# Expert rows stored already scaled by norm_moe, w1 and w3 loaded two rows per partition, and another arena order, in a two-block transformer kernel

## Chip, cores and metric

The kernel runs on one core of one Trainium2 chip, as one launch. The metric is the device time of that launch in microseconds; the time of a version is the median of several runs. Lower is better.

## What is computed

Two transformer blocks follow each other on 1024 rows of 1024 float32 numbers. The first has a gated linear recurrence and a differential attention side by side, and then a mixture of 32 experts, of which each row takes two. The second has sliding-window and forgetting attention and a plain MLP. The part that is changed is the mixture of experts, which in the reference comes to this:

```python
xn = rms_norm(x, norm_moe)                      # x * rsqrt(mean(x*x) + eps) * norm_moe
g_sel, e_in_group = router(xn)                  # top-1 group, top-2 experts of 8 in it
for e in range(32):                             # rows tok with weights w, packed by expert
    hid = silu(xn[tok] @ w1[e]) * (xn[tok] @ w3[e])     # 1024 -> 512
    out[tok] += (hid @ w2[e]) * w                       # 512 -> 1024
x = x + out
```

## The kernel before, in words

The program is written as tasks (Python generators) with priorities. A planner runs them: class `Model` holds assumed costs, `Tasks.run` takes the task of the highest priority whose data are due, and `Later` holds an instruction of ACT, DVE or POOL back until its operands are due by the model. So the order on each engine is a result of the planner, not of the text. Every matmul is issued in the helper's line 234, every ACT, DVE and POOL operation in line 270, plain DMAs in 221 and indirect ones in 227; in the profile the tile names tell the operations apart.

Products are made in three matmuls (`mm3`): each float32 operand is cut into a high part (float32r) and the rest. Weights come through one stream (`Stream`): a 512-KB piece is loaded from HBM into a raw buffer, cut (`split`: an ACT copy of 128x1024 makes the high part, a DVE subtract of 128x1024 the rest), and then used by PE. The raw buffers lie in the arenas `exact` (F) and two `swing` arenas, the cut ones in `rounded` (R). A load is issued when a raw buffer is free, a cut when a cut buffer is.

Phase `mix` (line 1297) multiplies the mixed branches with w_out, adds x and gets eight tiles of 128 rows. It stores each tile twice: to `XR` (d_xr), from which the experts' rows are gathered, and to `X1` (d_x), to which the experts' results are added by scatter. Meanwhile the router and the routing tables are computed.

Phase `moe` (line 1637) goes through the experts in the order of `moe_order` (line 605). For expert e, `hidden` takes the eight pieces of w1 and w3, 48 matmuls of 128x512; `xform` for the next expert turns the 128 gathered rows (eight transposes of 128x128 into PSUM) and cuts them into th and tl; `outputs` for the expert before takes four pieces of w2, 24 matmuls and a scatter; `turn` makes four transposes of the hidden rows. The gain norm_moe is applied in `xform`: after the transposes it is one number per partition (`self.gm`, one column for each 128 rows of the weights), so each 128x128 block has an ACT activation with that scale and a DVE scalar_tensor_tensor with it (`split_T`, line 653). The factor rsqrt of each row is applied later in `hidden` (`rt`). `gather` (line 1648) is an indirect DMA on POOL from XR. During the first experts DVE and PE also make the index tables of the later ones. `overflow` (line 1816) handles experts with more rows than one tile; its loop isn't entered here.

A piece of w1 or w3 holds 256 rows of 512 numbers; in `w_unit` (line 794) partition p gets rows p and 128+p, two runs of 2 KB. A piece of w2 holds 128 rows of 1024, one run of 4 KB for each partition.

Of the kernel before, what the change touches and what calls it, by code (L numbers as in the profile page):

```python
# [10 lines left out]
F32 = mybir.dt.float32  # L11
# [8 lines left out]
D = 1024  # L20
# [592 lines left out]
class Kern:  # L613
    def __init__(self, ctx, tc, io, out, stop=None):
# [5 lines left out]
        ps = ctx.enter_context(tc.tile_pool(name="ps", bufs=1, space=bass.MemoryType.PSUM))  # L620
        self.dram = ctx.enter_context(tc.tile_pool(name="dr", bufs=1, space=bass.MemoryType.DRAM))
        self.sz = ctx.enter_context(tc.tile_pool(name="sz", bufs=1, reuse_waits="tile"))
        self.R = Arena(sb.tile([128, NR], F32R, name="rounded"), NR, F32R)
        self.Z, self.turns = [None, None], 0
        for i in range(2):
            self.swing(i, F32R)
        self.F = Arena(sb.tile([128, NF], F32, name="exact"), NF, F32)
        self.psum = ps.tile([128, 4096], F32, name="psum")
# [165 lines left out]
    def w_unit(self, w, c0, n=512, k0=0, nk=8, kk=2):  # L794

        return [self.ws.add([(0, n, w[(k0 + i) * 128:(k0 + i + kk) * 128, c0:c0 + n].rearrange("(a p) c -> p a c", p=128))],
                            (kk, n)) for i in range(0, nk, kk)]

    def w_unit2(self, w, cols, nk=8, kk=2):

        out = []
        for i in range(0, nk, kk):
            at, srcs = 0, []
            for c, n in cols:
                srcs.append((at, n, w[i * 128:(i + kk) * 128, c:c + n].rearrange("(a p) c -> p a c", p=128)))
                at += n
            out.append(self.ws.add(srcs, (kk, at)))
        return out

    def plan(self):  # L810
# [15 lines left out]
        for kind, e in moe_order():  # L826
            if kind == "h":
                U["h"][e] = [self.w_unit(w[e], 0, k0=2 * i, nk=2)[0] for i in range(4) for w in (w1, w3)]
            if kind == "y":
# [467 lines left out]
    def mix(self):  # L1297
# [6 lines left out]
        self.x1 = Slots(F, 2, 1024)  # L1304
        self.x1ready = {}
        tb = Banks(self.psum, 4, 2)
        banks = Banks(self.psum, 0, 4)
# [46 lines left out]
        for half in range(2):  # L1354
# [39 lines left out]
            for tt in range(4 * half, 4 * half + 4):  # L1394
                b = yield from self.x1.take()
                self.sp.dma_start(b.f(), io["x"][0, tt * 128:(tt + 1) * 128])
                for u in range(2):
# [15 lines left out]
                    self.x1ready[tt, u] = b  # L1413
                for z in (self.XR, self.X1):
                    self.sp.dma_start(z[tt * 128:(tt + 1) * 128], b.f())
        mixT.free()
        self.swing(1, F32)
        self.ws.grow(raw=[self.Z[1].alloc(1024) for _ in range(2)])
# [218 lines left out]
    def moe(self):  # L1637
# [46 lines left out]
        def xform(e):  # L1684
# [3 lines left out]
            for c in range(2):  # L1688
                p = tb.next()
                self.transposes(p, x.f()[:, c * 512:c * 512 + 512], 4)  # L1690
                for j in range(4):
                    k = 4 * c + j
                    s = slice(k * 128, k * 128 + 128)
                    self.split_T(p[:, j * 128:j * 128 + 128], th.r()[:, s], tl.r()[:, s], th.f()[:, s], self.gm[:, k:k + 1])
            XT[e] = th.r(8, 128), tl.r(8, 128)
# [120 lines left out]
    def overflow(self, hl, th, tl, hT):  # L1816
# [29 lines left out]
        with tc.For_i(0, count, 1) as j:  # L1846
# [8 lines left out]
            for c in range(2):  # L1855
                p = self.bank(4 + c)
                transposes(p, xg.f()[:, c * 512:c * 512 + 512], 4)
                for i in range(4):
                    k = 4 * c + i
                    s, q, g = slice(k * 128, k * 128 + 128), p[:, i * 128:i * 128 + 128], self.gm[:, k:k + 1]  # L1860
                    act.activation(th.r()[:, s], q, AF.Copy, scale=g)
                    v.scalar_tensor_tensor(tl.r()[:, s], q, g, th.f()[:, s], op0=OP.mult, op1=OP.subtract)
            xh, xl = th.r(8, 128), tl.r(8, 128)
            for i in range(4):
                for n, w in enumerate((io["w1"], io["w3"])):
                    wh, wl = weights(w[0][bass.ds(e, 1), 256 * i:256 * i + 256].rearrange("o (a p) c -> p (o a) c", p=128), (2, 512))
                    for q in range(2):
# [759 lines left out]
```

## Time and profile before

| | |
|---|---|
| median of 3 runs | 2845.98 us (2844.07 to 2849.95) |
| the profiled execution | 2842.55 us |
| its span | 2840.6 us |
| mean granted TensorE clock | 0.981 |
| busy share | PE 95%, DVE 61%, ACT 53%, POOL 15% |
| DMA | 492.57 MB, mean 173 GB/s |

The span is from the first instruction to the last of one execution taken by the profiler; the execution's own time is a little longer. The experts take the stretch from about 932 to 1550 us of it; before it lies the first block's attention, behind it the second block. Times within the trace are counted from the start of the span. An idle time "[x <-E]" in a row is how long that engine had stood before it, and which engine's instruction ended the wait.

### The profile page before, as it was taken

How to read it: one execution, taken by the hardware profiler on the slowest of the kernel's cores; microseconds unless marked ns; L12 is line 12 of the kernel's file. 1: busy time of each engine (PE TensorE's matmuls, PEld its weight loads, DVE VectorE, ACT ScalarE, POOL GpSimd, SP SyncE). 2: the span in 40 equal slices, each digit the busy share in tenths (PEclk: the TensorE clock that was granted, in tenths of full speed). 3: DMA queues.
4: the chain of work that ended last, by engine and by line, in shares of the span. 5: the costliest groups of instructions: out<-in, count | busy, mean ns of one | idle time of the engine just before them, and what ended most of it. 6: DMA issues, size and time to landing. Idle time of an engine off the chain costs nothing. (4 is left out here: it accounts for less than half of the span.)

```text
span 2840.6 us, 37526 instructions
## 1 busy us (share of the span) xinstructions
PE 2692.9 (95%) x13162; PEld 2163.3 (76%) x13162; DVE 1738.8 (61%) x3243; ACT 1505.1 (53%) x2596; POOL 437.1 (15%) x486
## 2 busy tenths in 40 slices
PE   8899999999999899999998898899999999999999
PEld 6677787778777677788876776677777778888887
DVE  4474443643565798999997647846666665434333
ACT  4144444643443777899887646635545554243332
POOL 0540002420121232111111322200000100000000
PEclk9999999999999899999999999999999999999999
DMA  5322223335546898999997544353244433432321
GB/s 182 115 92 90 90 72 114 119 112 184 182 163 249 300 316 309 362 356 350 354 349 271 177 143 136 120 178 123 82 137 144 137 120 125 147 94 89 104 89 60
DMA packets 303023, 492.57 MB, mean 173 GB/s; under 512 B 30224, under 2 KB 127152, under 8 KB 302832
## 3 DMA queue, kind: packets, MB, share of 16 engines
q1 hardware_dynamic: 291136, 467.58, 48.2%
q0 software_dynamic: 9216, 16.81, 2.4%
q10 hardware_dynamic: 2480, 5.77, 0.5%
q8 instruction: 104, 1.70, 0.2%
q14 instruction: 87, 0.71, 0.1%
HBM read 436.38 MB, written 70.45 MB: 178 GB/s over the span
## 5 line engine op out<-in xcount | busy, mean ns | idle before, releaser
L234 PE MATMUL psum<-rounded,swing 128*128 128x512 f32 (+1 forms) x3840 | 945.0, 398 | 22.0 <-DVE exact L270 9.9
L234 PEld LDWEIGHTS psum<-rounded,swing 128*128 128x128 f32 x3840 | 704.1, 191 | 186.3 <-issue 17.7
L234 PE MATMUL psum<-swing,rounded 128*128 128x512 f32 (+2 forms) x3328 | 798.3, 393 | 0.0
L234 PE MATMUL psum<-rounded 128*128 128x512 f32 (+4 forms) x3456 | 750.6, 388 | 34.6 <-DVE rounded L270 15.3
L234 PEld LDWEIGHTS psum<-swing,rounded 128*128 128x128 f32 x3328 | 606.1, 189 | 141.3 <-issue 7.7
L234 PEld LDWEIGHTS psum<-rounded 128*128 128x128 f32 (+1 forms) x3456 | 572.9, 190 | 183.1 <-DVE rounded L270 23.6
L270 DVE TENSOR_TENSOR rounded<-exact,rounded 128x1024 fp32r<-128x1024 f32 (+2 forms) x477 | 557.2, 1191 | 239.9 <-ACT rounded L270 220.6
L270 ACT ACTIVATE rounded<-exact 128x1024 fp32r<-128x1024 f32 (+2 forms) x477 | 485.0, 1045 | 338.0 <-PE psum L234 291.8
L234 PE MATMUL psum<-exact 128*128 128x128 f32 (+5 forms) x2198 | 312.1, 284 | 79.1 <-DVE exact L270 23.3
L270 POOL TENSOR_TENSOR exact<-exact 128x1 f32<-128x1 f32 (+6 forms) x272 | 263.8, 973 | 714.4 <-DMA exact<-d_cb 287.6
L234 PEld LDWEIGHTS psum<-exact 128*128 128x128 f32 (+2 forms) x2198 | 261.8, 163 | 143.5 <-DVE exact L270 37.6
L270 ACT ACTIVATE exact<-psum 128x512 f32<-128x512 f32 (+4 forms) x282 | 155.2, 551 | 389.9 <-PE psum L234 322.1
L270 ACT ACTIVATE exact<-exact 128x512 f32<-128x512 f32 (+11 forms) x430 | 267.4, 632 | 166.1 <-DVE exact L270 136.8
L270 DVE TENSOR_TENSOR exact<-psum,exact 128x512 f32<-128x512 f32 x184 | 126.7, 688 | 200.9 <-PE psum L234 169.0
L270 DVE TENSOR_TENSOR rounded<-swing,rounded 128x1024 fp32r<-128x1024 f32 x196 | 228.9, 1217 | 11.9 <-ACT rounded L270 11.8
L270 ACT ACTIVATE rounded<-swing 128x1024 fp32r<-128x1024 f32 x196 | 201.1, 1089 | 26.1 <-PE psum L234 18.4
L270 DVE CUSTOM_DVE_ANT_0 exact<-psum,exact 128x512 f32<-128x512 f32 (+5 forms) x224 | 127.7, 592 | 71.1 <-PE psum L234 49.4
L270 POOL TENSOR_SCALAR exact<-exact 128x1 f32<-128x1 f32 (+4 forms) x134 | 41.7, 311 | 802.1 <-DVE exact L270 551.6
L270 DVE TENSOR_TENSOR swing<-psum,swing 128x512 fp32r<-128x512 f32 (+2 forms) x151 | 89.0, 615 | 90.1 <-ACT swing L270 89.8
L227 POOL DMA_INDIRECT d_x<-exact x31 | 67.3, 2172 | 482.3 <-ACT exact L270 482.3
L270 DVE TENSOR_TENSOR exact<-exact 128x512 f32<-128x512 f32 (+9 forms) x206 | 109.5, 538 | 46.9 <-POOL exact L270 24.0
L270 ACT ACTIVATE exact<-psum,exact 128x512 f32<-128x512 f32 (+1 forms) x174 | 95.2, 600 | 71.6 <-PE psum L234 60.9
(43 smaller groups left out, 1157.2 us busy)
## 6 DMA issues: line engine op xcount, KB each, us to landing
swing<-in_w_dram SPq DMA_DIRECT2D x192, 512.0 KB, 11.0
exact<-in_w_dram SPq DMA_DIRECT2D x181, 512.0 KB, 10.2
exact<-in_w_in_dram SPq DMA_DIRECT2D x72, 512.0 KB, 4.5
exact<-in_w_up_dram SPq DMA_DIRECT2D x64, 512.0 KB, 3.9
exact<-in_w_down_dram SPq DMA_DIRECT2D x64, 512.0 KB, 3.5
exact<-in_w_out_dram SPq DMA_DIRECT2D x32, 512.0 KB, 4.9
exact<-in_x_dram SPq DMA_DIRECT2D x16, 512.0 KB, 5.9
d_g<-exact SPq DMA_DIRECT2D x32, 256.0 KB, 2.3
```

The source lines that it names most:

```text
L227: r = fn(*args, **kw)
L234: r = fn(*args, **kw)
L270: r = fn(*args, **kw)
```

## The change

Four things are changed.

The arena `exact` moves to a pool of its own behind the swing arenas. Its size and use stay.

The rows of XR are stored multiplied with norm_moe. `mix` loads norm_moe once to all partitions (`xgain`, 512 KB) and multiplies every row tile on DVE (128x1024) into a new buffer `xgr` before the store to XR. X1 gets the plain rows as before. So `xform` no longer applies a gain, and cuts 512 columns at a time: two ACT copies and two DVE subtracts of 128x512 for an expert, in place of eight and eight of 128x128.

A piece of w1 or w3 is loaded so that partition p gets rows 2p and 2p+1, one run of 4 KB (`w_pair`). The k-th part of the sum then runs over the even or the odd rows of a block of 256. To match, XR's columns are stored in that order (`pairs`): within each 256, first the even ones, then the odd ones.

`overflow` is changed in the same way. `xgain` and `xgr` hold 2048 columns of `exact` during `mix`; in the experts' phase the stream has 24 raw buffers where it had 25. On POOL the order is the same.

The core of the diff (`overflow` left out):

```diff
@@ __init__ @@
+        self.R = Arena(sb.tile([128, NR], F32R, name="rounded"), NR, F32R)
         self.sz = ctx.enter_context(tc.tile_pool(name="sz", bufs=1, reuse_waits="tile"))
-        self.R = Arena(sb.tile([128, NR], F32R, name="rounded"), NR, F32R)
         self.Z, self.turns = [None, None], 0
         for i in range(2):
             self.swing(i, F32R)
-        self.F = Arena(sb.tile([128, NF], F32, name="exact"), NF, F32)
+        sf = ctx.enter_context(tc.tile_pool(name="sf", bufs=1))
+        self.F = Arena(sf.tile([128, NF], F32, name="exact"), NF, F32)
...
+    def w_pair(self, w, k0):
+
+        return self.ws.add([(0, 512, w[k0:k0 + 256].rearrange("(p a) c -> p a c", a=2))], (2, 512))
...
-                U["h"][e] = [self.w_unit(w[e], 0, k0=2 * i, nk=2)[0] for i in range(4) for w in (w1, w3)]
+                U["h"][e] = [self.w_pair(w[e], 256 * i) for i in range(4) for w in (w1, w3)]
@@ mix @@
+        self.xgain, xgr = F.alloc(1024), Ring(F, 1, 1024)
+        self.sp.dma_start(self.xgain.f(), self.row_bcast(io["norm_moe"], D))
+        pairs = lambda z: z.rearrange("p (i q a) -> p i a q", a=2, q=128)
...
-                for z in (self.XR, self.X1):
-                    self.sp.dma_start(z[tt * 128:(tt + 1) * 128], b.f())
+                xg = xgr.next()
+                v.tensor_tensor(xg.f(4, 2, 128), pairs(b.f()), pairs(self.xgain.f()), OP.mult)
+                self.sp.dma_start(self.XR[tt * 128:(tt + 1) * 128], xg.f())
+                self.sp.dma_start(self.X1[tt * 128:(tt + 1) * 128], b.f())
         mixT.free()
+        self.xgain.free()
+        xgr.free()
@@ moe, xform @@
                 p = tb.next()
-                self.transposes(p, x.f()[:, c * 512:c * 512 + 512], 4)
-                for j in range(4):
-                    k = 4 * c + j
-                    s = slice(k * 128, k * 128 + 128)
-                    self.split_T(p[:, j * 128:j * 128 + 128], th.r()[:, s], tl.r()[:, s], th.f()[:, s], self.gm[:, k:k + 1])
+                s = slice(c * 512, c * 512 + 512)
+                self.transposes(p, x.f()[:, s], 4)
+                self.split(p, th.r()[:, s], tl.r()[:, s], th.f()[:, s])
```

Since the planner sets the order, these are three places at which it differs.

The first is ACT while the experts' tables are made, at one of five experts at which it stood in this way. `rounded` from `psum` is xform's or turn's high part, `rounded` from `exact` or `swing` a piece of weights; the brackets name the engine or queue whose semaphore is waited for. Before:

```order
L270 ACTIVATE swing_6227<-psum,exact 128x512
L270 ACTIVATE rounded<-psum,exact 128x128 [waits PE_49]
L270 ACTIVATE rounded<-psum,exact 128x128 [waits DVE_49] x3
L270 ACTIVATE rounded<-psum,exact 128x128 [waits PE_49]
L270 ACTIVATE rounded<-psum,exact 128x128 [waits DVE_49] x3
L270 ACTIVATE rounded<-exact 128x1024 [waits DMAHW2_49,PE_49,Activation_49]
L270 ACTIVATE rounded<-exact 128x1024 [waits DMAHW3_49,PE_49,Activation_49]
L270 ACTIVATE rounded<-swing_6227 128x1024 [waits DMAHW4_49,PE_49,Activation_49]
L270 ACTIVATE rounded<-swing_6227 128x1024 [waits DMAHW5_49,PE_49,Activation_49]
L270 ACTIVATE exact<-psum,exact 128x512 [waits DMASW6_49]
L270 ACTIVATE exact<-psum,exact 128x512
L270 ACTIVATE rounded<-psum 128x512 [waits PE_49]
```

and now:

```order
L270 ACTIVATE swing_6241<-psum,exact 128x512
L270 ACTIVATE rounded<-exact 128x1024 [waits DMAHW2_49,DVE_49,PE_49]
L270 ACTIVATE rounded<-psum 128x512 [waits PE_49] x2
L270 ACTIVATE rounded<-swing_6241 128x1024 [waits DMAHW3_49,DVE_49,PE_49]
L270 ACTIVATE rounded<-swing_6241 128x1024 [waits DMAHW4_49,DVE_49,PE_49]
L270 ACTIVATE rounded<-swing_6241 128x1024 [waits DMAHW5_49,DVE_49,PE_49]
L270 ACTIVATE exact<-psum,exact 128x512 [waits DMASW2_49,PE_49]
L270 ACTIVATE exact<-psum,exact 128x512 [waits PE_49]
L270 ACTIVATE rounded<-psum 128x512 [waits PE_49]
```

Of xform's rows (128x128 with `psum`, now the pair of 128x512), three of each four activations waited for DVE; the two that stand now wait for PE alone.

The second is SP at the last row tile of `mix`; the loads of weights stand between the stores to d_xr and d_x. Before:

```order
L221 DMA exact<-in_w_dram 128x1024 x4
L221 DMA swing_6227<-in_w_dram 128x2x512 x2
L221 DMA d_xr<-exact 128x1024
L221 DMA d_x_4488<-exact 128x1024
L221 DMA exact<-in_w_dram 128x2x512
L221 DMA swing_5792<-in_w_dram 128x2x512 x6
```

and now:

```order
L221 DMA swing_6241<-in_w_dram 128x1024 x2
L221 DMA d_x_4491<-exact 128x1024
L221 DMA exact<-in_w_dram 128x1024
L221 DMA d_xr<-exact 128x1024
L221 DMA swing_5800<-in_w_dram 128x1024 x6
```

The store to d_xr now stands behind the store to d_x and one more load.

The third is DVE at the same tile. Before:

```order
L270 TENSOR_TENSOR exact<-psum,exact 128x512
L270 TENSOR_TENSOR rounded<-exact,rounded 128x1024
L270 SCALAR_TENSOR_TENSOR exact<-exact 128x1
L270 RECIPROCAL exact<-exact 128x1
L270 TENSOR_TENSOR exact<-exact 128x1
L270 TENSOR_SCALAR exact<-exact 128x32 x2
L270 TENSOR_TENSOR exact<-exact 128x1
L270 TENSOR_TENSOR exact<-exact,psum 128x96
```

and now:

```order
L270 TENSOR_TENSOR exact<-psum,exact 128x512
L270 TENSOR_TENSOR rounded<-exact,rounded 128x1024
L270 SCALAR_TENSOR_TENSOR exact<-exact 128x1
L270 TENSOR_TENSOR exact<-exact 128x1024
L270 TENSOR_TENSOR exact<-exact 128x1
L270 RECIPROCAL exact<-exact 128x1
L270 TENSOR_TENSOR exact<-exact 128x1
L270 TENSOR_SCALAR exact<-exact 128x32 x2
L270 TENSOR_TENSOR exact<-exact,psum 128x96
```

The multiply exact<-exact of 128x1024 stands between the steps of the last tile's routing.

Beside these, nine transposes in the second block's attention on PE, which stood behind 21 matmuls of one product, now stand behind 66; some 150 us later the rows are the same again.

## Rows read from the trace of the kernel before

**Rows 1.** Windows: stage, its length, busy time of each engine, TensorE clock, DMA, GB/s.

```profile
1002.00:1157.00 155.00, 138.80 (x621) 111.23 (x620) 138.75 (x237) 114.77 (x168) 35.37 (x15) 0.94 0.88 309
1157.00:1405.00 248.00, 248.00 (x1178) 206.31 (x1177) 238.57 (x309) 226.25 (x336) 42.38 (x28) 1.00 0.99 358
1405.00:1517.00 112.00, 108.75 (x504) 87.40 (x503) 100.06 (x131) 95.01 (x144) 17.04 (x11) 1.00 0.98 356
1850.00:2310.00 460.00, 442.80 (x2234) 351.90 (x2233) 288.44 (x576) 234.03 (x435) 26.63 (x43) 0.98 0.43 133
```

**Rows 2.** PE in time, steady expert: start, duration, operation, count, idle before.

```profile
1157.11 1.04 PE L234 MATMUL psum<-exact 128*128 128x128 f32 x8
...
1163.80 11.15 PE L234 MATMUL psum<-rounded 128*128 128x512 f32 x48
1174.79 1.03 PE L234 MATMUL psum<-exact 128*128 128x128 f32 x8
```

**Rows 3.** PE in time, 1002 to 1157 us.

```profile
1001.67 1.04 PE L234 MATMUL psum<-exact,swing 128*128 128x128 f32 x8
...
1077.21 0.66 PE L234 MATMUL psum<-exact 128*128 128x48 f32 x2 [2.31 <-DVE exact L270]
1077.65 11.49 PE L234 MATMUL psum<-rounded 128*128 128x512 f32 x36
```

**Rows 4.** Groups by shape, 1002 to 1157: busy us, mean ns, idle before.

```profile
L234 PE MATMUL psum<-rounded 128*128 128x512 f32 x504 | 130.3, 413 | 9.3 <-ACT rounded L270 5.0 <-DVE rounded L270 4.2
...
L270 ACT ACTIVATE rounded<-psum,exact 128x128 fp32r<-128x128 f32 x56 | 18.4, 372 | 28.0 <-DVE rounded L270 28.0
L270 DVE SCALAR_TENSOR_TENSOR rounded<-psum,exact,rounded 128x128 fp32r<-128x128 f32 x56 | 18.0, 346 | 13.7 <-ACT rounded L270 13.7
```

**Rows 5.** DVE in time, one expert's xform.

```profile
1047.07 0.34 DVE L270 SCALAR_TENSOR_TENSOR rounded<-psum,exact,rounded 128x128 fp32r<-128x128 f32 x1
1047.85 0.35 DVE L270 SCALAR_TENSOR_TENSOR rounded<-psum,exact,rounded 128x128 fp32r<-128x128 f32 x1 [0.44 <-ACT rounded L270]
...
1052.31 1.22 DVE L270 TENSOR_TENSOR rounded<-exact,rounded 128x1024 fp32r<-128x1024 f32 x1
```

**Rows 6.** ACT in time, the same xform.

```profile
1048.24 0.37 ACT L270 ACTIVATE rounded<-psum,exact 128x128 fp32r<-128x128 f32 x1 [0.42 <-DVE rounded L270]
```

**Rows 7.** Groups by shape, 1157 to 1405.

```profile
L234 PE MATMUL psum<-rounded 128*128 128x512 f32 x1010 | 237.0, 392 | 0.0
...
L270 DVE SCALAR_TENSOR_TENSOR rounded<-psum,exact,rounded 128x128 fp32r<-128x128 f32 x112 | 30.1, 340 | 0.0
...
L270 DVE TENSOR_TENSOR rounded<-psum,rounded 128x512 fp32r<-128x512 f32 x14 | 9.6, 683 | 0.0
```

**Rows 8.** PE in time, 1405 to 1518.

```profile
1405.03 1.04 PE L234 MATMUL psum<-exact,swing 128*128 128x128 f32 x8
...
1486.98 0.66 PE L234 MATMUL psum<-exact,swing 128*128 128x128 f32 x4 [1.63 <-DVE swing L270]
...
1517.24 0.93 PE L234 MATMUL psum<-exact,swing 128*128 128x128 f32 x7
```

**Rows 9.** DMA, 1160.5 to 1162 (4-KB rows) and 1166 to 1169.5 (2-KB rows).

```profile
DMA packets 167, 0.62 MB, mean 412 GB/s; under 512 B 17, under 2 KB 17, under 8 KB 166
...
DMA packets 720, 1.38 MB, mean 395 GB/s; under 512 B 45, under 2 KB 45, under 8 KB 720
```

**Rows 10.** Groups by shape, 700 to 918.

```profile
L270 DVE TENSOR_TENSOR rounded<-exact,rounded 128x1024 fp32r<-128x1024 f32 x30 | 36.6, 1225 | 11.2 <-ACT rounded L270 11.2
```

**Rows 11.** PE in time, start of the experts.

```profile
931.79 1.97 PE L234 MATMUL psum<-exact 128*128 128x128 f32 x8 [4.41 <-DMA exact<-d_xr,exact]
```

**Rows 12.** Answer for the tile d_xr: issue to landing.

```profile
DMA to landing us min/median/max: 4.3/8.7/13.2
```

**Rows 13.** ACT's queue in time, start of the experts.

```profile
935.89 7.73 ACTq L221 DMA_DIRECT2D exact<-in_w_dram  x7
```

**Rows 14.** PE in time, attention of the second block.

```profile
1952.86 0.74 PE L234 MATMUL psum<-exact 128*128 128x128 f32 x5 [2.15 <-DMA exact<-d_kva]
```

More of the change, by code (lines that the diff above doesn't have):

```diff
@@ L1856, in overflow @@
                 p = self.bank(4 + c)
[L1857 to L1862, printed above, removed]
+                s = slice(c * 512, c * 512 + 512)
+                transposes(p, xg.f()[:, s], 4)
+                split(p, th.r()[:, s], tl.r()[:, s], th.f()[:, s])
             xh, xl = th.r(8, 128), tl.r(8, 128)
@@ L1865, in overflow @@
                 for n, w in enumerate((io["w1"], io["w3"])):
-                    wh, wl = weights(w[0][bass.ds(e, 1), 256 * i:256 * i + 256].rearrange("o (a p) c -> p (o a) c", p=128), (2, 512))
+                    wh, wl = weights(w[0][bass.ds(e, 1), 256 * i:256 * i + 256].rearrange("o (p a) c -> p (o a) c", a=2), (2, 512))
                     for q in range(2):
```

## The prediction, made before the changed kernel was run

> **What bounds the kernel now.** I read the busy time by stage first, then PE's own line of time in the expert stage, then DVE and ACT at the places where PE stood still, and last the DMA. The windows [rows 1] cut the 32 experts into pieces. From 1157 to 1405 us PE is busy 248.00 of 248.00 us. There one expert costs PE 17.68 us, from one row of eight transposes to the next (1157.11 to 1174.79) [rows 2]; a DVE or ACT saving there buys nothing. From 1002 to 1157 it is different: seven experts, whose first transposes start at 1001.67 and whose successor's at 1157.11 [rows 2, 3], take 155.4 us, 22.2 each, while seven of the steady kind would take 123.8. In this stretch PE is busy 138.80 of 155, DVE 138.75, ACT 114.77, at a mean granted clock of 0.94. So 31.6 us lie in this stretch, some 5 to 10 of them in 16 pairs of small table matmuls of 128x48 that stand only there (one pair is in [rows 3], 0.66 us), and the question is who holds PE for the rest.
>
> PE's rows show pauses that end on DVE or ACT, one of them 2.31 us [rows 3, 4], and behind it the lower clock: 36 matmuls take 11.49 us (319 ns each) where the steady stage does 48 in 11.15 (232 ns each) [rows 2, 3]. DVE itself looks only 90% busy, but by shape its idle time has one owner: the 56 scalar_tensor_tensor of 128x128 by which xform cuts the turned rows into two parts were preceded by 13.7 us of waiting for ACT, and ACT's 56 activations of the same tile by 28.0 us of waiting for DVE [rows 4]. Time order shows why. In five of the seven experts the two engines work hand over hand: DVE's block at 1047.07, the next at 1047.85, with 0.44 us of waiting for ACT, and ACT's with 0.42 us of waiting for DVE, pitch 0.78 us, until DVE's next piece of weights at 1052.31 [rows 5, 6]: 5.2 us for eight blocks, when eight blocks of 0.27 net are 2.15 without the waits (30.1 us for 112 in the steady stage [rows 7]). Busy and waiting together, DVE accounts for 138.75 + 13.7 = 152.45 of 155 us. **DVE is the bound of this stretch**, and over two fifths of its xform time there (13.7 of 31.7) is the hand-off.
>
> **The change part by part.** *xform.* Eight activations and eight scalar_tensor_tensor of 128x128 become two activations and two tensor_tensor of 128x512. The hand-off can't stand in the new order: the ACT rows shown above have lost the wait for DVE and wait for PE alone. So DVE's 13.7 us of waiting go. Its work goes from 18.0 us [rows 4] to 14 tensor_tensor of the form already there, 683 ns each [rows 7], 9.6 us: 8.4 less. By DVE's account the stretch needs 155 − 22.1 = 132.9 us. PE's account: it has 16.2 us of pauses to give, and 504 matmuls that took 413 ns instead of 392 [rows 4, 7], 10.6 us, most of it lower clock after pauses; it can't go below 138.80 − 10.6 = 128.2. At the clock of now it would need 138.8. I take −18, between PE at the clock of now (−16.2) and DVE's account (−22.1), since the clock comes back only where a pause is gone. The lower end is −8.4, when the 13.7 us of hand-off are only exchanged for other waits. In the 14 experts from 1157 to 1405 PE has no pause, so the 0.8 us less of DVE in each (2.15 less 2 x 0.683) is worth 0 there.
>
> Can the weights follow? The stretch moves 309 GB/s x 155 us = 47.9 MB; at the 358 GB/s of the next stage [rows 1] this takes 133.8 us. So the gain of 18 is not given back by an emptier stock; one of 22 nearly would be.
>
> *Pair loads.* From 1405 PE waits again, now because raw pieces run out: six experts from 1405.03 to 1517.24 take 112.2 us instead of 106.1, with waits as at 1486.98 [rows 8]. 6.1 us can be had back. A window with 167 packets for 0.62 MB, so 4-KB rows nearly alone, moved 412 GB/s, one with 720 for 1.38 MB, 2-KB rows, 395 [rows 9]: 4% for two thirds of the bytes is 2.9%, and an expert's twelve pieces, 6.29 MB at 356 GB/s [rows 1], are 17.7 us, so 0.5 us per expert, 10 us in the 20 experts from 1157 to 1517 against a loss of 6.1. Against it: one raw buffer fewer (24 for 25), worth one piece, 1.5 us. The window sums are rough (0.62 MB), so I take −2; ends −6 and +2. The Trainium skill (DMA: Bandwidth & Descriptors, Specifications) speaks against any gain from it: line rate needs 512 B per transfer, and both row lengths are above. By it this term would be 0 or the lost buffer's +1.5, and the sum 2 to 3.5 us higher.
>
> *Row scaling.* Eight multiplies of 128x1024 on DVE; the nearest row is 1225 ns [rows 10], the new ones read with a stride of two, for which I allow up to twice that. Seven lie under PE work in a stretch where DVE is idle nearly half the time: 0. The eighth is in front of the first gather. XR's last tile is now stored behind the multiply, one more weight piece and X1's store, as the SP rows show. PE's first expert transposes stand at 931.79 after 4.41 us of waiting for that gather [rows 11]. The multiply comes between DVE's routing steps too, and pushes all of them by 1.2. I take +1.5 (multiply 1.2, a little for the queue); ends 0, if the store lands as fast as the shortest of its queue, and +6: landings to and from d_xr, stores and gathers together, range from 4.3 to 13.2 us around 8.7 [rows 12], which is +4.5, and 1.2 of the multiply.
>
> *Ramp.* ACT issues seven loads in 7.73 us at 935.89 and stands in its own queue meanwhile [rows 13]; now one load fewer is issued there, and most with half the packets. −1; ends 0 and −4.
>
> *Block 2.* The planner interleaves its attention a little differently between 1950 and 2310 us; the transposes that waited 2.15 us for d_kva at 1952.86 [rows 14] now have 45 more matmuls ahead. From 1850 to 2310 PE is busy 442.80 of 460 us [rows 1], most of the rest before the moved place, so it could win 4 at most, and moved work may lose as much: 0, ends −4 and +6. *Layout.* Only addresses move and no instruction is placed otherwise by it: 0.
>
> The sum: −18 − 2 + 1.5 − 1 + 0 = −19.5 us. The profiled execution took 2842.55 us, 2.0 more than its span; it lies 3.4 under the median of the runs, 2845.98. On the median I predict **2826.5 us**.
>
> **The rivals.** (a) *The stream gains nothing by 4-KB rows.* The mechanism is: experts reach 1405 18 us earlier at an unchanged rate and with one buffer less. For it: the DMA is at 0.98 to 0.99 in these stages [rows 1], and the two windows differ by 4% only. The loss of 6.1 then stays and grows by 1.5, and if half of the stock was built in the pauses that go, by 3 more: −18 + 1.5 − 1 + 4.5 = −13, 2833. It is what the rule named above comes to here.
> (b) *Hand-off time moves.* DVE stands in the same list of splits and table steps; relieved of ACT's wait it meets the next (the pauses of PE on the experts' tables, as 2.31 us at 1077.21 [rows 3], end on DVE whatever xform does). Then only the shorter work counts, 8.4 less the late start of 1.5: 2839.
> (c) *No change.* The change does what it says to xform and not what that is for: in these seven experts DVE also builds the experts' tables, and PE's table matmuls (the 2.31 us of [rows 3]) wait for those. If the tables set the pace, the relieved 22 us of DVE only become waiting for PE. DVE's account, 152.45 of 155, leaves just 2.55 us of such waiting now and speaks against it; for it speaks that PE's longest pauses are at tables. With the late start and the ramp it comes to 2846.
> (d) *Slower.* The late store of XR's last tile. The gather waits for its landing; if this is one of the slow ones (+4.5), behind multiply (+1.2) and one more piece (+1.5), PE stands 7.2 us longer, and all experts with it. It decides if the relief in the stretch is below about 1.5: 2853. Against it: the median landing and the trace's own wait of 4.41 us leave it at +1.5 in the usual case.
>
> **How the numbers follow.** Chances: forecast 0.55, (a) 0.15, (b) 0.14, (c) 0.09, (d) 0.07. A measurement of this kernel can tell about 0.2%, 5.7 us: below 2840.3 is faster, above 2851.7 slower. Faster: the forecast, (a) and half of (b): 0.77. Same: the other half of (b), and (c): 0.16. Slower: (d), 0.07. The range: the low end takes DVE's account (−22.1), the tail's whole 6.1 and a ramp of −4 without a late start, −32: 2814; the high end reaches through (a) and (b) to 2844, short of (c) and (d).
>
> **What would show it.** Right: in the changed profile, ACT's and DVE's rounded<-psum of 128x512 stand without a hand-off and no row with scalar_tensor_tensor of 128x128 is left; the seven experts take 134 to 140 us, with DVE busy over 93% and the granted clock at 0.96 or more; the first gather starts 1 to 3 us later relative to the last in-tile of the stage before; the last six experts lose less than 6. Wrong: the stretch still takes 150 us with DVE waiting for ACT or for something else, or the experts from 1157 on take more than 17.7 us each because pieces land late, or the first transposes come more than 5 us later.

## The result and the profile after

The changed kernel takes 2802.11 us (median of 4 runs, 2800.13 to 2804.50) against 2846.47 us of the kernel before: 44.4 us less, ratio 0.9844 with a 95% interval of 0.9827 to 0.9861. The forecast was 2826.5 us, range 2814 to 2844. The direction was right, and the gain was over twice as large as the 19.5 us that were forecast.

The page of the changed kernel begins:

```profile
span 2799.5 us, 37151 instructions
...
PE 2664.0 (95%) x13162; PEld 2164.8 (77%) x13162; DVE 1721.3 (61%) x3059; ACT 1478.9 (53%) x2404; POOL 428.5 (15%) x486
...
DMA packets 270397, 493.08 MB, mean 176 GB/s; under 512 B 30240, under 2 KB 127168, under 8 KB 270208
```

Its span is 41.1 us shorter than the 2840.6 us before, the DMA's packets are 270,397 (303,023 before, by the same line of its page), and the bytes are the same but for the broadcast of norm_moe. Where the 41.1 us went is read from the starts of PE's rows, each place as the distance between two starts, so that a shift further ahead doesn't enter:

| place (PE's rows) | before | after | difference | forecast |
|---|---|---|---|---|
| start to the first expert's transposes | 931.8 | 929.6 | −2.2 | +1.5 |
| first to fifth expert | 69.9 | 67.1 | −2.8 | −1 |
| fifth to twelfth, the experts with tables | 155.4 | 132.8 | −22.7 | −18 |
| twelfth to last | 360.1 | 357.8 | −2.3 | −2 |
| last expert to the second block's first transposes | 43.2 | 43.3 | 0 | 0 |
| from there to the end of the span | 1280.1 | 1268.9 | −11.2 | 0 |

The starts of the first expert, of the last and of the second block, where rows above don't show them; the first line is of the kernel before, the others of the changed one:

```profile
1560.48 2.10 PE L234 MATMUL psum<-exact 128*128 128x128 f32 x8 [10.74 <-DMA exact<-d_x]
```

```profile
929.58 1.97 PE L234 MATMUL psum<-exact 128*128 128x128 f32 x8 [4.39 <-DMA exact<-d_xr,exact]
...
1487.32 1.04 PE L234 MATMUL psum<-exact,swing 128*128 128x128 f32 x8
...
1530.63 2.26 PE L234 MATMUL psum<-exact 128*128 128x128 f32 x8 [10.89 <-DMA exact<-d_x]
```

Four places moved in the direction of the forecast, or not at all where that was forecast; of these the stretch with the tables lies 4.7 us from its value. The start and the second block did not: they gave 13.4 us, where +1.5 and 0 were forecast.

**The experts.** The windows of the changed kernel for the seven experts and for the last six, and PE's rows at the seven experts' ends, with the one pause between them, which answer to [rows 1 to 3] and [rows 8]:

```profile
996.70:1129.48 132.78, 129.87 (x623) 108.02 (x622) 130.31 (x195) 109.11 (x127) 39.53 (x14) 0.99 0.98 360
1377.54:1487.32 109.78, 107.17 (x505) 88.09 (x504) 95.90 (x95) 88.66 (x108) 18.14 (x11) 1.00 0.98 360
```

```profile
996.70 1.03 PE L234 MATMUL psum<-exact,swing 128*128 128x128 f32 x8
...
1012.29 0.42 PE L234 MATMUL psum<-exact 128*128 128x48 f32 x2 [2.92 <-DVE exact L270]
...
1129.48 1.04 PE L234 MATMUL psum<-exact 128*128 128x128 f32 x8
...
1147.21 1.03 PE L234 MATMUL psum<-exact 128*128 128x128 f32 x8
```

DVE is busy 130.31 of 132.78 us, 98%, but it no longer sets the pace: PE is busy 129.87 us, as much, and its only pause in the stretch is the one of 2.92 us at 1012.29; from 1057.34 to the end of the stretch it has none. PE's own account of the stretch, against this line of the kernel before, is the whole gain: its pauses fell from 16.2 to 2.9 us, and its busy time from 139.24 to 129.87, with the granted clock at 0.99 for 0.95.

```profile
1001.67:1157.11 155.44, 139.24 (x623) 111.59 (x622) 139.19 (x237) 115.11 (x168) 35.70 (x15) 0.95 0.88 309
```

By shape, against [rows 4]:

```profile
L234 PE MATMUL psum<-rounded 128*128 128x512 f32 x505 | 123.5, 399 | 0.0
...
L270 DVE TENSOR_TENSOR rounded<-psum,rounded 128x512 fp32r<-128x512 f32 x21 | 13.8, 681 | 0.0
L270 ACT ACTIVATE rounded<-psum 128x512 fp32r<-128x512 f32 x21 | 11.7, 594 | 0.0
```

No idle time stands at either form (seven of the 21 are `turn`'s, the other 14 are xform's), and in time the two blocks follow each other, 1.28 us for both, where [rows 5] showed 5.2 us for eight:

```profile
1041.24 1.28 DVE L270 TENSOR_TENSOR rounded<-psum,rounded 128x512 fp32r<-128x512 f32 x2
```

**The second block.** There the order of most matmuls is as before, and the MLP's is the same throughout. The rows of PE in the MLP, first of the kernel before, then of the changed one:

```profile
2513.19 21.97 PE L234 MATMUL psum<-rounded 128*128 128x512 f32 x96
2535.00 22.55 PE L234 MATMUL psum<-swing,rounded 128*128 128x512 f32 x96
2557.39 22.56 PE L234 MATMUL psum<-rounded,swing 128*128 128x512 f32 x96
2579.79 22.56 PE L234 MATMUL psum<-swing,rounded 128*128 128x512 f32 x96
```

```profile
2478.89 21.92 PE L234 MATMUL psum<-rounded 128*128 128x512 f32 x96
2500.65 21.92 PE L234 MATMUL psum<-swing,rounded 128*128 128x512 f32 x96
2522.41 21.92 PE L234 MATMUL psum<-rounded,swing 128*128 128x512 f32 x96
2544.17 21.92 PE L234 MATMUL psum<-swing,rounded 128*128 128x512 f32 x96
```

The names are moving operand, stationary operand. From one start to the next, 96 matmuls with one operand in a swing arena took 22.39 us before, 233.2 ns each, and 21.76 us now, 226.7 ns; the row with both operands in `rounded` took 21.81 and 21.76. So the same instructions in the same order take 2.8% less time where they read swing. Nothing in the change touches them but the place of the arenas.

### The profile page after: what moved, and what is told of

The parts are those of the page before. It is cut to its first block, busy times and chain, and to the rows that moved or that the text cites. A ratio compares the mean times of both kernels' runs of the same rounds, so it can differ in the third digit from the quotient of the medians.

```text
span 2799.5 us, 37151 instructions
## 1 busy us (share of the span) xinstructions
PE 2664.0 (95%) x13162; PEld 2164.8 (77%) x13162; DVE 1721.3 (61%) x3059; ACT 1478.9 (53%) x2404; POOL 428.5 (15%) x486
## 2 busy tenths in 40 slices
DMA packets 270397, 493.08 MB, mean 176 GB/s; under 512 B 30240, under 2 KB 127168, under 8 KB 270208
## 5 line engine op out<-in xcount | busy, mean ns | idle before, releaser
L234 PE MATMUL psum<-swing,rounded 128*128 128x512 f32 (+1 forms) x3328 | 784.8, 389 | 0.8 <-DVE exact L270 0.4
L234 PE MATMUL psum<-rounded 128*128 128x512 f32 (+4 forms) x3456 | 740.9, 386 | 23.9 <-DVE rounded L270 9.6
L270 DVE TENSOR_TENSOR rounded<-exact,rounded 128x1024 fp32r<-128x1024 f32 (+2 forms) x483 | 565.8, 1193 | 227.8 <-ACT rounded L270 220.5
L270 ACT ACTIVATE rounded<-exact 128x1024 fp32r<-128x1024 f32 (+2 forms) x483 | 496.4, 1035 | 380.9 <-PE psum L234 313.7
L234 PE MATMUL psum<-exact 128*128 128x128 f32 (+6 forms) x2198 | 316.7, 286 | 80.3 <-DVE exact L270 25.2
L270 ACT ACTIVATE rounded<-swing 128x1024 fp32r<-128x1024 f32 x190 | 195.4, 1067 | 15.1 <-PE psum L234 12.3
L270 DVE TENSOR_TENSOR exact<-exact 128x512 f32<-128x512 f32 (+9 forms) x214 | 119.6, 566 | 41.7 <-POOL exact L270 24.3
L270 ACT ACTIVATE rounded<-psum 128x512 fp32r<-128x512 f32 (+2 forms) x190 | 88.3, 496 | 104.6 <-PE psum L234 103.9
L270 DVE TENSOR_TENSOR rounded<-psum,rounded 128x512 fp32r<-128x512 f32 (+2 forms) x190 | 101.7, 558 | 58.8 <-ACT rounded L270 58.6
```

The source lines that it names most:

```text
L234: r = fn(*args, **kw)
L270: r = fn(*args, **kw)
```

## The experiments

Kernels that are compared ran on one chip, beside the kernel before. Ratios are to that kernel's runs there; where its median is named, it is that one. Single executions, the profiled ones too, lie several us around a median, so places are compared by their own lengths; the profiled execution of the kernel before, 2842.55 us, lies 5 to 6 us below its medians in these comparisons (2847.37 to 2848.75), so spans show less of a gain than medians.

### The layout alone, and all but the layout

`e_layout` is the kernel before with this part of the change alone:

```diff
+        self.R = Arena(sb.tile([128, NR], F32R, name="rounded"), NR, F32R)
         self.sz = ctx.enter_context(tc.tile_pool(name="sz", bufs=1, reuse_waits="tile"))
-        self.R = Arena(sb.tile([128, NR], F32R, name="rounded"), NR, F32R)
...
-        self.F = Arena(sb.tile([128, NF], F32, name="exact"), NF, F32)
+        sf = ctx.enter_context(tc.tile_pool(name="sf", bufs=1))
+        self.F = Arena(sf.tile([128, NF], F32, name="exact"), NF, F32)
```

> The kernel before with nothing changed but the place of the arenas (exact behind the two swing arenas). The order on every engine is that of before. Theory A (the operands' places in SBUF cost PE time): 13 to 17 us less than before, about 5 of them ahead of 930 us and 9 to 11 behind 1560, and in the MLP 96 matmuls with an operand in swing take 21.9 us as those with both in rounded, where before showed 22.55; the experts from 932 to 1550 keep their 618 us. Theory B (addresses cost nothing, the second block's gain came from the planner's other order there): within 4 us of before, and the 96 matmuls at 22.5.

Measured: 2831.15 us against 2848.75, 17.6 less, ratio 0.9933 (0.9911 to 0.9955). From the second block's first transposes to the end it takes 1268.9 us, to a tenth what the changed kernel takes, and the first expert starts at 927.8, 4.0 earlier than before; the seven experts still take 155.5 us. In the MLP the 96 matmuls with swing are down to 21.92 us:

```profile
2532.81 21.92 PE L234 MATMUL psum<-swing,rounded 128*128 128x512 f32 x96
```

`e_nolayout` is the changed kernel with these lines put back.

> The changed kernel with the arenas where they were before: scaled rows, wide xform and pair loads without the layout. Theory A: 25 to 31 us less than before (so 13 to 17 more than the changed kernel); 96 matmuls of the MLP with swing at 22.55 us; seven experts after the fourth take 131 to 136 us. Theory B: the time of the changed kernel, 2802, within 4 us.

Measured: 2818.72 us, 30.0 less than before, ratio 0.9899 (0.9880 to 0.9918). The seven experts take 132.7 us, the second block 1280.4 as before, and the first expert starts at 932.9, 1.1 later than before. Theory A holds in both runs, `e_layout` 0.6 us beyond its range: the layout is worth some 17 us, the rest 30, and together they make up the change within the runs' spread. One part went otherwise: in `e_layout` the 20 experts from the twelfth to the last take 364.8 us, 4.6 more than before. They begin earlier there, and the last one begins at 1518.2, as before (1517.2). So of the layout's 17.6 us the two profiled executions show 9.4, the difference of their spans: 11.2 in the second block and 4.0 at the start, less what the experts lose; the rest lies in no place that they show.

### What about the place costs PE time

The first probe has seven buffers a to g, each 29,760 bytes of a partition behind the one before, and takes the stationary and the moving operand from each pair.

```python
for n in range(49):                      # stationary n // 7, moving n % 7
    for m in range(48):
        l = 128 * (m // 3 % 2 * 2 + (m % 3 == 2))
        matmul(acc, t[n // 7][:, l:l + 128], t[n % 7][:, 448:960] if m % 3 == 1 else t[n % 7][:, 512:1024], ...)
```

> A probe, not the kernel: it computes nothing of the reference. Seven buffers a to g lie one behind the other in SBUF, 29,760 bytes of each partition apart. For each of 49 pairs PE does 48 matmuls of 128x512 in float32r, the stationary operand out of one buffer and the moving operand out of the other, with nothing beside them; then 16 of the pairs (a, c, e, g) again while ACT and DVE write pieces into a. Theory A (far place): matmuls with an operand in the last two or three buffers take 6 to 7 ns more each, whatever the other operand is. Theory B (distance): they do so only if the two operands lie more than about four buffers apart, so that g with g is as fast as a with a. Theory C (traffic): all 49 pairs are alike, 228 to 230 ns from one matmul to the next, and a difference shows only beside ACT and DVE.

None of the three theories held. PE's rows, stationary operand a, then the first ones of b; and, last, four of the rows beside ACT and DVE:

```profile
18.88 11.17 PE L36 MATMUL psum<-sbb,sba 128*128 128x512 f32 x48
29.88 11.32 PE L36 MATMUL psum<-sbc,sba 128*128 128x512 f32 x48
41.04 11.36 PE L36 MATMUL psum<-sbd,sba 128*128 128x512 f32 x48
52.24 11.06 PE L36 MATMUL psum<-sbe,sba 128*128 128x512 f32 x48
63.14 11.17 PE L36 MATMUL psum<-sbf,sba 128*128 128x512 f32 x48
74.14 11.32 PE L36 MATMUL psum<-sbg,sba 128*128 128x512 f32 x48
85.30 11.36 PE L36 MATMUL psum<-sba,sbb 128*128 128x512 f32 x48
96.50 11.06 PE L36 MATMUL psum<-sbb 128*128 128x512 f32 x48
107.40 11.17 PE L36 MATMUL psum<-sbc,sbb 128*128 128x512 f32 x48
...
129.56 11.36 PE L36 MATMUL psum<-sbe,sbb 128*128 128x512 f32 x48
140.76 11.06 PE L36 MATMUL psum<-sbf,sbb 128*128 128x512 f32 x48
...
561.00 11.35 PE L36 MATMUL psum<-sbc,sba 128*128 128x512 f32 x48
572.19 11.06 PE L36 MATMUL psum<-sbe,sba 128*128 128x512 f32 x48
583.09 11.35 PE L36 MATMUL psum<-sbg,sba 128*128 128x512 f32 x48
594.28 11.36 PE L36 MATMUL psum<-sba,sbc 128*128 128x512 f32 x48
```

From start to start: with a stationary, moving b takes 11.00 us, c 11.16, d 11.20, e 10.90, f 11.00, g 11.16. With b stationary, a takes 11.20 and b 10.90, and e is slow (11.20) which was fast with a. So neither a far place nor the distance as such decides, and the traffic changes next to nothing (beside it c with a takes 11.19 us, e with a 10.90). The times come back with every fourth buffer, and 4 x 29,760 is 465 x 256: 29,760 is 64 modulo 256. Ordered by the difference of the two addresses (moving less stationary) modulo 256, all pairs but the first, whose 48 matmuls took 13.85 us, fall on four levels: 0 takes 10.90 to 10.93 us, 227 ns a matmul; 64 takes 10.99 to 11.01; 128 takes 11.15 to 11.20; 192 takes 11.19 to 11.20, 233 ns.

The arenas fit. Before, `rounded` begins at 16512 and the swing arenas at 163584 and 196352: 128 and 0 modulo 256. In the changed kernel swing begins at 84096 and 116864, both 128, as `rounded` does. The reason is `exact`, whose 19,872 columns are 79,488 bytes, 310.5 times 256; it stood between them and now stands behind.

```python
for n in range(33):                      # w and m begin at the same address modulo 256
    group(4 * n, n % 7, 512)             # 48 matmuls, moving operand at m[:, 1024 + 4 * n:]
    group(4 * n, 7, 256)
```

> A second probe, not the kernel: 48 matmuls of 128x512, then 48 of 128x256, with the stationary operand at one place and the moving operand moved on by 16 bytes from group to group, 33 groups of each, 0 to 512 bytes. Theory A (the distance between the operands modulo 256 bytes decides): the time of a group has a period of 256 bytes, 11.06 us at 0, 256 and 512, 11.17 at 64, 11.3 to 11.4 at 128 and 192. Theory B (only the place of the moving operand, or a period of 512 or more): no repetition at 256.

In the second probe the groups follow each other without a gap, so the profile merges them into one row; these are the distances from the first matmul of a group of 512 columns to the first of the next group, from the starts in the trace. Offset 0 took 10.880; it stands behind a group of 512 columns, all others behind one of 256.

```
offset of the moving operand, bytes : us for 48 matmuls
  16 11.127   32 11.200   48 11.191   64 10.991   80 11.085   96 11.199  112 11.094
 128 11.160  144 11.203  160 11.237  176 11.197  192 11.202  208 11.261  224 11.199  240 11.352
 256 10.925
 272 11.127  288 11.200  304 11.191  320 10.991  336 11.086  352 11.199  368 11.093
 384 11.160  400 11.203  416 11.236  432 11.197  448 11.203  464 11.260  480 11.199  496 11.352
 512 10.924
```

The period is 256 bytes: from 16 to 240 every offset takes the same time at 256 more, to a nanosecond for the 48. Theory A holds, though its values don't. The times of 11.06, 11.17 and 11.3 to 11.4 that were expected are those of the rows, whose end reaches into the next group; from start to start the first probe's four levels were 10.90, 11.00, 11.16 and 11.20, and here 0, 64, 128 and 192 give 10.92, 10.99, 11.16 and 11.20. What is read together, so that this difference counts, was not found out.

Two kernels test it in place. `e_pad` is the kernel before with one line, `e_shift` the changed kernel with the same line behind `rounded`:

```diff
         self.F = Arena(sb.tile([128, NF], F32, name="exact"), NF, F32)
+        sb.tile([128, 32], F32, name="pad")
```

> The kernel before with 128 unused bytes between exact and the swing arenas, and nothing else: the arenas stay in their order, far from each other, but rounded and swing now begin at the same address modulo 256 (16512 and 163712, 128 both; before, 163584 gave 0). Theory A (modulo 256): the whole effect of the layout without the move: 13 to 19 us less than before, 96 matmuls of the MLP with swing at 21.9 us. Theory B (nearness or low addresses): within 4 us of before, and 22.55 us.

> The changed kernel with 128 unused bytes between rounded and the swing arenas: the same order of arenas, swing at 84224 in place of 84096, so 0 modulo 256 against 128 of rounded. Theory A: the layout's effect is lost, 2815 to 2821 us as without the layout, 96 matmuls at 22.55 us. Theory B: as the changed kernel, 2802 within 4 us.

Measured: `e_pad` 2832.18 us against 2848.52, 16.3 less, ratio 0.9937 (0.9913 to 0.9961); `e_shift` 2823.79 us, 21.7 more than the changed kernel's 2802.11 (which ran at another time; the ratio to before is 0.9897, 0.9871 to 0.9924, as without the layout). Rows of PE in the MLP, `e_pad` and `e_shift`:

```profile
2532.82 21.92 PE L234 MATMUL psum<-swing,rounded 128*128 128x512 f32 x96
2554.58 21.92 PE L234 MATMUL psum<-rounded,swing 128*128 128x512 f32 x96
```

```profile
2517.10 22.55 PE L234 MATMUL psum<-swing,rounded 128*128 128x512 f32 x96
2539.49 22.56 PE L234 MATMUL psum<-rounded,swing 128*128 128x512 f32 x96
```

Theory A holds in both directions: 128 unused bytes do what the move of the arena did, and undo it. `e_shift` lies 2.8 us above the range that was given for it.

### The experts' parts

`e_scale` takes the changed kernel without the layout and puts back the loads of w1 and w3 and the order of the columns, in `overflow` too (left out here):

```diff
...
-                U["h"][e] = [self.w_pair(w[e], 256 * i) for i in range(4) for w in (w1, w3)]
+                U["h"][e] = [self.w_unit(w[e], 0, k0=2 * i, nk=2)[0] for i in range(4) for w in (w1, w3)]
...
-                v.tensor_tensor(xg.f(4, 2, 128), pairs(b.f()), pairs(self.xgain.f()), OP.mult)
+                v.tensor_tensor(xg.f(), b.f(), self.xgain.f(), OP.mult)
```

> The kernel before with scaled rows and the wide xform alone: w1 and w3 are loaded as before, XR's columns stay in their order, the arenas are where they were. Theory A (DVE bounds the seven experts of the tables, and the hand-off with ACT is its loss): the stretch takes 132 to 137 us where before took 155.4, and the kernel 20 to 27 us less than before; the last six experts lose 6 us or more against the steady 17.7 each. Theory B (the loads with 4-KB rows made the stretch and the ramp shorter): the stretch stays above 145 us, the kernel within 10 us of before.

Measured: 2829.60 us, 19.2 less, ratio 0.9935 (0.9914 to 0.9957). The seven experts take 131.8 us: theory A, with the stretch 0.2 us below what it gave and the kernel's gain 0.9 us short of it; the last six experts lose 9.3 us. Here are the starts of its twelfth and last expert, and of the same experts in `e_nolayout`, which differs from it by the pair loads:

```profile
1133.16 1.03 PE L234 MATMUL psum<-exact 128*128 128x128 f32 x8
...
1498.75 1.03 PE L234 MATMUL psum<-exact,swing 128*128 128x128 f32 x8
```

```profile
1134.20 1.03 PE L234 MATMUL psum<-exact 128*128 128x128 f32 x8
...
1491.42 1.03 PE L234 MATMUL psum<-exact,swing 128*128 128x128 f32 x8
```

Twelfth to last takes 365.6 us with 2-KB rows and 357.2 with 4-KB rows; before it was 360.1. So of the 23.6 us that the stretch gave, 5.5 were lost again where the weights run out, and the waits begin at the 24th expert (1346 us) where before they began at the 27th (1423). The pair loads won back 8.4 us, not 2.

`e_pair` has the pair loads alone, on the kernel before (`w_pair` itself is as in the change):

```diff
...
-                U["h"][e] = [self.w_unit(w[e], 0, k0=2 * i, nk=2)[0] for i in range(4) for w in (w1, w3)]
+                U["h"][e] = [self.w_pair(w[e], 256 * i) for i in range(4) for w in (w1, w3)]
```

> The kernel before with the pair loads of w1 and w3 alone; XR's columns are not reordered, so the products of the experts pair the wrong rows (the same amount of work). Orders as before. Theory A (the 4-KB rows make the stream faster): the stretch with the tables stays at 153 to 157 us, as DVE bounds it, the last six experts lose 0 to 3 us instead of 6, the kernel 3 to 8 us less than before. Theory B (4-KB rows are no faster than 2-KB rows): within 2 us of before, and the last six experts take 112 us as they did.

Measured: 2840.12 us against 2847.95, ratio 0.9973 (0.9963 to 0.9982): 7.8 less by the medians, while the profiled execution's span is 2.6 shorter. Its seven experts take 155.3 us, twelfth to last 355.6 against 360.1, 4.5 less. Theory A holds: 4-KB rows do load faster. The DMA's lines for 1157 to 1405 us, before and `e_pair`:

```profile
DMA packets 39177, 88.73 MB, mean 358 GB/s; under 512 B 4611, under 2 KB 4611, under 8 KB 39155
```

```profile
DMA packets 26733, 90.56 MB, mean 365 GB/s; under 512 B 4670, under 2 KB 4670, under 8 KB 26711
```

365 against 358 GB/s is 2.0%, with a third fewer packets, where [rows 9] had been taken for 2.9%. The Trainium skill (DMA: Bandwidth & Descriptors, Specifications) has 512 B as the least transfer for line rate, and 358 GB/s as HBM's limit per core; by the first, e_pair would have been at 358 too. These lines show 2% above, and the measurement decides here.

`e_hand` keeps the small blocks and their gain on the kernel before, and only writes four activations ahead of four scalar_tensor_tensor:

```diff
                 for j in range(4):
                     k = 4 * c + j
                     s = slice(k * 128, k * 128 + 128)
-                    self.split_T(p[:, j * 128:j * 128 + 128], th.r()[:, s], tl.r()[:, s], th.f()[:, s], self.gm[:, k:k + 1])
+                    act.activation(th.r()[:, s], p[:, j * 128:j * 128 + 128], AF.Copy, scale=self.gm[:, k:k + 1])
+                for j in range(4):
+                    k = 4 * c + j
+                    s = slice(k * 128, k * 128 + 128)
+                    v.scalar_tensor_tensor(tl.r()[:, s], p[:, j * 128:j * 128 + 128], self.gm[:, k:k + 1], th.f()[:, s], op0=OP.mult, op1=OP.subtract)
```

> The kernel before with the same eight activations and eight scalar_tensor_tensor of 128x128 per expert, but four activations written ahead of four scalar_tensor_tensor, so that ACT no longer waits for DVE between them; arenas, loads and gain as before. Theory A (the hand-off waits are the loss): DVE's 13.7 us of waiting go, its work stays: the stretch takes 139 to 145 us, the kernel 10 to 16 less than before. Theory B (the work of the small blocks is the loss, the waits would have been spent elsewhere): the stretch stays above 150 us and the kernel within 5 us of before.

Measured: 2824.95 us against 2848.75, 23.8 less, ratio 0.9922 (0.9898 to 0.9946): theory A, and more than it gave for the stretch and for the kernel. Its seven experts:

```profile
998.22:1133.84 135.62, 131.47 (x624) 108.62 (x622) 133.80 (x236) 114.93 (x168) 48.37 (x15) 0.97 0.97 349
```

```profile
L270 ACT ACTIVATE rounded<-psum,exact 128x128 fp32r<-128x128 f32 x56 | 15.2, 389 | 0.0
...
L270 DVE SCALAR_TENSOR_TENSOR rounded<-psum,exact,rounded 128x128 fp32r<-128x128 f32 x56 | 15.3, 346 | 0.7 <-ACT rounded L270 0.7
```

135.6 us, 19.8 less than before, with the same 56 small blocks. DVE's wait at them fell from 13.7 to 0.7 us, ACT's from 28.0 to nothing, and the blocks themselves cost 15.3 in place of 18.0 us, as they overlap when they follow each other. By DVE's rows the order alone gave back 13.0 us of waiting and 2.7 of work, and the wide blocks could save some 6 of work more (15.3 less the 9.2 of 14 wide ones, two thirds of 13.8). By the stretch the order counts for more: it alone makes the stretch 19.8 us shorter, and the wide blocks of `e_scale` (131.8 us) another 3.8.

`e_hand_pad` joins `e_hand` and `e_pad`; the changed kernel was run again beside it, and `e_early`, the changed kernel with the multiply in two halves:

```diff
-                xg = xgr.next()
-                v.tensor_tensor(xg.f(4, 2, 128), pairs(b.f()), pairs(self.xgain.f()), OP.mult)
+                    if not u:
+                        xg = xgr.next()
+                    h = slice(u * 512, u * 512 + 512)
+                    v.tensor_tensor(xg.f()[:, h].rearrange("p (i a q) -> p i a q", a=2, q=128), pairs(x), pairs(self.xgain.f()[:, h]), OP.mult)
```

> The kernel before with the two small edits that the runs so far point to, and none of the changed data: 128 unused bytes in front of the swing arenas, and in xform four activations ahead of four scalar_tensor_tensor. If the two effects add (24 and 16 us in their own runs): 2805 to 2813 us, MLP 96 matmuls at 21.9 us, the table stretch 134 to 137 us, and more waiting for weights behind 1320 us than in the changed kernel, as the rows of w1 and w3 stay at 2 KB. If they overlap: above 2815.

> The changed kernel itself again, for a comparison on one chip with the two others of this call: 2798 to 2806 us; the stretch of the seven experts 132 to 134 us.

> The changed kernel with the multiply by norm_moe made in two halves, each as soon as its half of the row tile is there, so that XR's last tile can be stored some 0.6 us earlier. If the late store holds the first gather: the first expert's transposes 0.5 to 2 us earlier than in the changed kernel and the total lower by as much, which these rounds can't tell from nothing; if the gather waits for the index or for the queue, no change of that place. The planner's order changes elsewhere too, which may cost or give 5 us.

Measured together, against 2847.37 us: `e_hand_pad` 2808.78, ratio 0.9860 (0.9836 to 0.9884); the changed kernel 2800.91, 0.9821 (0.9781 to 0.9860); `e_early` 2801.64, 0.9828 (0.9801 to 0.9855). The two small edits add up and give 38.6 of 46.5 us; the seven experts take 134.7 us, and what is missing is in the last experts, 367.9 us from the twelfth to the last (357.9 in the changed kernel beside it). In `e_early` the first expert starts at 927.0, in the changed kernel beside it at 928.7. That is within what was expected, but the start alone moves as much from run to run: the rerun's lies 0.8 ahead of the first run's, and the two runs with the layout alone and with the pad, whose orders are the same, differ by 1.0. No version was found that is faster than the changed kernel beyond doubt.

## Why the prediction was wrong, point by point

**The step that failed** is the shortest one: "Only addresses move and no instruction is placed otherwise by it: 0." It measured 17.6 us alone (`e_layout`), and 128 bytes of padding measured 16.3 (`e_pad`); by place 11.2 in the second block and some 4 ahead of the experts are to be seen. The inference from an unchanged order to an unchanged time left out that an instruction may take another time at another address. The trace of before had the sign of it: 96 matmuls with both operands in `rounded` in 21.81 us and with one in swing in 22.39, in neighbouring rows of PE. These rows weren't among those that the argument read: none of its rows is of the MLP.

**The bound of the stretch** was right for the kernel before: DVE with its hand-off. The account of 22.1 us measured 22.7 in the changed kernel and 23.6 in `e_scale`, so the seven experts lie just below the 134 to 140 us that were named as the sign. The value taken was −18, on the doubt that PE's clock would come back; it came back to 0.99 and 1.00. By PE's account, 13.3 of its 16.2 us of pauses went and 9.4 us of its busy time, where 10.6 had been the most, and what is left is PE's own work and one pause. The split of DVE's account, 13.7 of waiting and 8.4 of work, was wrong: the order alone took 19.8 us off the stretch (`e_hand`), the wide blocks 3.8 more (`e_scale`). A part of the work was the hand-off's too, as small blocks don't overlap in it: 18.0 us for 56 of them, 15.3 without it.

**Pair loads and the stock.** The stock is the weights that are loaded ahead. That the gain of 18 "is not given back by an emptier stock" was wrong: `e_hand`, whose loads are those of before, gains 19.8 us and gives 2.8 of them back from the twelfth expert to the last, and `e_scale` 5.5 of 23.6. The loads' 133.8 us, which the sentence went by, allow nothing to be lost in the first (135.6 us) and 2.0 in the second (131.8). The term of −2 came out as −2.3 in net, but as −8.4 for the loads and +5.5 for the stock; both were sized too small, and of the lost buffer nothing can be told apart. From the 26th expert six take 109.8 us, 3.7 over the steady time, where 6 were named as the limit. Rival (a) falls: the rows of 4 KB are 2% faster.

**Row scaling.** +1.5 for the late store; without the layout the first expert started 1.1 us later (`e_nolayout`), in `e_scale` 0.4, but in `e_pair`, which scales nothing, 1.2, so the runs don't tell the term from 0. The eight multiplies with a stride of two took 1224 ns in the mean, as the row without one did (1225 [rows 10]). In the changed kernel PE waits 4.39 us for the first gather, 4.41 before [rows 11]. Rival (d) falls.

**The ramp.** −1 was forecast, 2.8 measured between the first and the fifth expert. In `e_nolayout` the same distance is 68.7 us and in `e_scale` 69.2, in the second run of the changed kernel 68.7, against 69.9 before: some 1 us, and the rest is within what two runs differ by. `e_hand` has the loads of before and takes 68.4, so that this 1 us comes from the loads is not shown.

**Rivals (b) and (c)** fall with `e_scale` and `e_hand`: the relief wasn't only exchanged for the next wait, and the tables didn't set the pace. One wait of that kind is left, 2.9 us at 1012, as 3.4 us before.

With the layout's 17 us set aside, 2818.7 us remain (`e_nolayout`): inside the range, 8 us below the value. As a difference to the kernel before it is 30.0 us by the medians and 25.0 by the spans, where 19.5 were forecast; the stretch with the tables is the largest part of that difference, −22.8 for −18. That the −2 of the pair loads came out is luck, as two larger terms of opposite sign make it up.

## What to carry to other kernels

Where an edit moves buffers, compare the time of one and the same matmul form by the pairs of buffers that it reads, row by row, before calling the move free; here arenas that begin at the same address modulo 256 bytes were worth some 17 us, and one padding of 128 bytes got 16.3 of them. Where two engines make a pair of results block by block, read the idle time by shape on both: a small wait on each side, at every block, is one hand-off that a longer run on the first engine removes. And when a stretch ahead of a stream's limit is shortened, count what it will take from the stock further on.

## What the runs showed of the hardware that was not expected

At a granted clock of 1.00 a float32r matmul of 128x512 took 227 to 236.5 ns, depending on the difference of its operands' addresses modulo 256 bytes: 227 to 228 at 0, 229 at 64, 232 to 233 at 128, 233 at 192 (`p_addr`, `p_step`) and 236.5 at 240 (`p_step`). At 0 and 128 it was the same with nothing else running and beside ACT and DVE (`p_addr`), and the 48 of a group repeat to a nanosecond at 256 bytes more (`p_step`). For 256 columns 48 matmuls took 5.44 to 5.76 us by the offset, with the lowest at 64, 112 and 192. DVE's blocks of 128x128 took 0.27 us each where they follow each other (`e_hand`, 15.3 us for 56), and 0.78 us where it and ACT wait for each other at every block (before, [rows 5]). And from 1157 to 1405 us the DMA engines moved 365 GB/s with the weights in rows of 4 KB (`e_pair`) and 358 with a mixture of 2 and 4 KB (before), both with the DMA engines busy 0.99 of the time.
